# A two-layer trunk on one core: the order in which down blocks add to x, and four more seven-product pairs

## The chip, the cores and the metric

One core of a Trainium2 chip runs one program. The metric is the device time of one execution in microseconds (us); lower is better. The kernel works on 256 tokens, and nearly all of its time goes into multiplying these by large weight matrices that are read once from memory.

## What is computed

The reference is a decoder trunk of two layers in float32 for x of shape (1, 256, 2048):

```python
for layer in range(DEPTH):
    xn = rms_norm(x, norm_mix[layer])
    if layer % 2 == 0:
        x = x + mixer_mlstm_ssd(xn, *mixer_params[layer])
    else:
        x = x + mixer_moba(xn, *mixer_params[layer])
    x = x + swiglu(rms_norm(x, norm_ffn[layer]), *ffn_params[layer])
return rms_norm(x, final_norm)

def swiglu(x, w_gate, w_up, w_down):
    return (jax.nn.silu(x @ w_gate) * (x @ w_up)) @ w_down
```

The change concerns the two `swiglu` parts, with a hidden width of 5632. The mixers (an mLSTM and a Mamba-2 group in layer 0, block-sparse attention in layer 1) stay as they are.

## The kernel before, in words

**Products.** All float32 products are made from a high part (`wh`, rounded to the type fp32r by ScalarE, L269) and the rest (`wl`, made by VectorE, L274). So each product is three matmuls: high x high, high x low, low x high (L305 to L307 of `add`).

**Blocks.** A block multiplies the 256 tokens (two tiles of 128) by two strips of 512 weight columns, so it has four results, each in a PSUM bank: F[0] to F[3] (`acc_f`, banks 0 to 3), F[2 t + s] for token tile t and strip s. The inner dimension is taken in pairs of 128 rows; each letter of a block's plan in `PLAN` is one pair. "P" is a plain pair: four results x two halves of the pair x three matmuls, 24 in all, results in the order 0, 2, 1, 3. "S" is a pair with seven products in place of eight (Strassen's scheme), 21 matmuls. Three of its products go straight into F[0] to F[2], and four into E banks (`acc_e`, banks 4 to 7). It needs sums of the activations (`sk`, made by `activation_sums`) and of the weights (`sums`). In the FFN the weight sums are made by transfers that accumulate in memory order: SP loads one part (L259), POOL issues another that is added (L260); two more weight tiles are formed on VectorE (L287, L289).

**Behind the last S pair** of a block the E banks are combined into four SBUF tiles `pre` (one on ScalarE at L338, four instructions on VectorE at L339 to L342). `pre` and F together give the block's result: F[i] + pre[i], with a minus for i = 2. `pre` comes from the pool `tmp`, which has nine buffers.

**Hidden and down blocks.** `ffn` walks over eleven strips of 512 hidden columns in groups of 4, 4 and 3. For each strip `hidden` runs a block of eight pairs on gate and up (plan "x0" for the first strip of a layer, "x" for the others) and makes h from it; its results come out through `gathered`, which puts F[i] + pre[i] into `pre` (L388) at high priority. Then `down` multiplies the group's strips by the down matrix in two blocks, q = 0 and q = 1, one for each half of x's columns: plans "down4" (eight pairs) and "down3" (six). Their results are added to x (`xin`) by `add_all`, at L919: once for the four tiles of `pre`, once for the four banks F. There are twelve down blocks. The very last one (layer 1, group of three, q = 1) is the tail: it takes two pairs at a time at its end and adds its banks one by one in `finish_last`, together with the final norm.

**Order.** The program is written in one order; a scheduler then fixes the order of each engine's queue ahead of the run, by its own estimates. Each instruction's rank comes from its place in the program. `tc.high_priority(offset=n)` moves it forward by n places. Weights are prepared at offset 800, the combinations of E and the adds of F at 1600. Within a queue an engine runs strictly as written.

**Deferred work.** `later(n, ...)` puts off small work (above all `transpose_split`, which turns finished parts of x or h into the next blocks' operand) by n pairs. It runs in `tick()`, after each pair. Between the first and the last S of a block it is held back (`held`), because it uses the same banks 4 to 7.

Of the kernel before, what the change touches and what calls it, by code (L numbers as in the profile page):

```python
# [23 lines left out]
STRIP = 512  # L24
# [12 lines left out]
PLAN = {  # L37
    "bc": "PPPPPPPP", "xz": "PPPPPPPP", "qk0": "PPPPPPPP", "w1": ("PSPSPSPP", "PSPSPSPP"),
    "v0": "PPPSPSPP", "o": "PPPSPSPP", "qk1": "PPPSPSPP", "v1": "PPPSPSPP", "w2": ("PPPSPSPP", "PPPSPSPP"),
    "x": "PSPSPSSP", "x0": "PPPSPSPP", "down4": ("PSPSPSSP", "PSPSPSSP"), "down3": ("PSPSPP", "PPPSPP"),  # L40
    "av0": "PPPSPSPP", "aq": "PPPSPSPP", "av1": "PPPSPSPP", "wo": ("PPPPPPPP", "PPPSPSPP"),
}

# [18 lines left out]
def hybrid_trunk(ctx: ExitStack, tc: tile.TileContext, a: dict, out: bass.AP):  # L62
# [23 lines left out]
    def t2(shape, name, dt=F32):  # L86
        return tmp.tile(shape, dt, tag="tmp", name=name, bufs=9)
# [71 lines left out]
    last, cast, nth, fresh = [None], [None], [None], [None, None]  # L159
# [85 lines left out]
    def turn_strip(kt, s, src, gcol, wait, step=0):  # L245
        for i in range(2):
            later(wait + i * step, (kt.name, 2 * s + i), transpose_split, kt, 2 * s + i,
                  [x[:, i * T:(i + 1) * T] for x in src], gcol)
# [133 lines left out]
    def gathered(F, pre):  # L382
        for i in (0, 2, 1, 3):
            if pre is None:
                yield i // 2, i % 2, F[i]
            else:
                with tc.high_priority(offset=1600):
                    (nc.vector.tensor_sub if i == 2 else nc.vector.tensor_add)(pre[i], F[i], pre[i])  # L388
                yield i // 2, i % 2, pre[i]
# [34 lines left out]
    def first_pair(src, turns_after, warm):  # L424
        raw = []
        for w, col in src:
            raw.append(home("raw")([P, 2, STRIP], "raw"))
            nc.sync.dma_start(raw[-1], w[:2 * P, col:col + STRIP].rearrange("(a p) f -> p a f", p=P))
        b = xt0.pair(0)
        pt = aux_bank("p_tr")  # L430
        with tc.issue_after(turns_after):
            for i in range(2):
                for t in range(NT):
                    turned = nc.tensor.transpose(pt[:, i * T + t * P:i * T + (t + 1) * P],
                                                 xin[t][:, i * P:(i + 1) * P], ident).ins
        with tc.issue_after(turned):
            warm_up(warm)
        pair = pt.rearrange("p (a b) -> p a b", a=2)
        high = [home("wh")([P, 2, STRIP], "wh", F32R) for _ in raw]
        low = [home("wl")([P, 2, STRIP], "wl", F32R) for _ in raw]  # L440

        def staged(s, k):
            with tied(last[0], cast[0]):
                split(high[s][:, k, :], low[s][:, k, :], raw[s][:, k, :])
            cast[0], last[0] = fresh

        for k in range(2):
            g = pv[:, G_MIX0 + k:G_MIX0 + k + 1]
            with tied(last[0], cast[0]) if k else ExitStack():
                split(b[:, k, 0, :], b[:, k, 1, :], pair[:, k, :], g)  # L450
            cast[0], last[0] = fresh
            staged(0, k)
        for k in range(2):
            staged(1, k)
        return [[(h[:, k, :], l[:, k, :]) for k in range(2)] for h, l in zip(high, low)]
# [57 lines left out]
    with tc.high_priority(offset=2000):  # L513
        first = first_pair(((w_in, C_B), (w_in, C_C)), rows_turned, WARM[1])
# [383 lines left out]
    def ffn(xt, r, wg_, wu_, wd, name, finish, begin=None):  # L898

        def hidden(hT, i, s, plan):  # L900
            F, pre = block(((wg_, s * STRIP), (wu_, s * STRIP)), xt, 0, plan)
            got = {(t, i): src for t, i, src in gathered(F, pre)}
            hs = []
            for t in range(NT):
                g, u = got[t, 0], got[t, 1]
                h = t2([P, STRIP], "h")
                nc.scalar.activation(h, g, AF.Silu, scale=r[:, t:t + 1])
                nc.vector.scalar_tensor_tensor(h, u, r[:, t:t + 1], h, op0=OP.mult, op1=OP.mult)
                hs.append(h)
            turn_strip(hT, i, hs, None, 1)  # L910

        def down(hT, first, n, last):
            for q in range(2):
                c0 = 2 * q * STRIP
                dst = [xr_[t][:, c0 + n_ * STRIP:c0 + (n_ + 1) * STRIP] for t in range(NT) for n_ in range(2)]

                def add_all(what, minus=None):
                    for i, (d, x) in enumerate(zip(dst, what)):
                        (nc.vector.tensor_sub if i == minus else nc.vector.tensor_add)(d, d, x)  # L919

                if last and begin is not None:
                    begin(2 * q)
                    begin(2 * q + 1)
                tail = last and q and name == "b"
                F, _ = block(((wd, c0), (wd, c0 + STRIP)), hT, first * STRIP, PLAN[f"down{n}"][q], lambda pre: add_all(pre, 2),
                             lead=2 if tail else 1, order=(0, 1, 2, 3) if tail else (0, 2, 1, 3))
                if tail:
                    finish_last(F)
                    continue
                with tc.high_priority(offset=1600):  # L930
                    add_all(F)
                if last:
                    for s in (2 * q, 2 * q + 1):
                        finish(s)

        in_transfers[0] = True
        first = 0
        for n in (4, 4, 3):
            over = s_home if n == 3 else sk_home
            hT = KT(f"h{name}{first}", 4 * n, s_home, {1: s_home, 3: over, 5: over, 6: s_home})  # L940
            hT.sums = {j: None for j in range(2 * n) if "S" in [p[j] for p in PLAN[f"down{n}"]]}
            for i in range(n):
                hidden(hT, i, first + i, PLAN["x" if first + i else "x0"])
            down(hT, first, n, first + n == DFF // STRIP)
            first += n
        in_transfers[0] = False
# [207 lines left out]
```

## Time and profile before

| what | value |
|---|---|
| median of three runs | 2567.0 us (2564.78 to 2567.02) |
| the profiled execution's own time | 2565.22 us |
| its span, first to last instruction | 2563.4 us |
| TensorE busy | 2541.0 us (99%) |
| VectorE (DVE) busy | 2226.2 us (87%) |
| ScalarE (ACT) busy | 1562.7 us (61%) |
| POOL busy | 276.4 us (11%) |
| read from memory | 586.17 MB |

PE is TensorE, DVE VectorE, ACT ScalarE; SP and POOL issue transfers. A row of the timeline gives the start and the duration in us, the engine, the source line, the operation, `out<-in` by tile names, the shape and the count; in brackets stands idle time before it and what ended that. Matmuls are pipelined, so the row of one overlaps the next, and the distance between two starts is what a product takes. A row of the windows gives the stretch, its length, then for PE, PEld (weight loads), DVE, ACT and POOL the busy time and the number of instructions that touch the stretch, then the granted TensorE clock (1.00 is full), the busy share of the DMA engines, and GB/s.

### The profile page before, as it was taken

The numbers are of one execution on the slowest core, as the hardware profiler recorded it, in microseconds if no ns is written. First come the engines' busy times: TensorE is split into PE (matmuls) and PEld (weight loads), VectorE is DVE, ScalarE is ACT, GpSimd is POOL, SyncE is SP. The second block draws the span as 40 slices with busy tenths as digits, with TensorE's granted clock in tenths as the row PEclk, the third lists the DMA queues.
The fourth block names the chain that finished last, engine by engine and source line by source line (L and its number), as shares of the span: only waits on it lengthen the run. The fifth ranks groups of instructions, "written<-read, shape, count | busy, mean of one in ns | idle before, by whom it ended". The sixth has DMA issues, their size and how long they took to land.

```text
span 2563.4 us, 33984 instructions
## 1 busy us (share of the span) xinstructions
PE 2541.0 (99%) x11607; PEld 2092.0 (82%) x11607; DVE 2226.2 (87%) x2979; ACT 1562.7 (61%) x2100; POOL 276.4 (11%) x348
## 2 busy tenths in 40 slices
PE   9999999999999999999999999999999999999998
PEld 7888888888888888788878888888888878887887
DVE  6877789887788999999999988887889999999898
ACT  6566765565666665666556655646666656665664
POOL 2101200000001111111111000000011111111110
PEclk9999999999999999999999999999999999999999
DMA  8656656566477999999999756455679999999894
GB/s 281 182 167 186 205 166 218 172 195 203 164 230 217 280 265 283 264 282 261 288 264 281 224 179 205 157 165 181 205 234 268 275 276 268 274 273 298 253 262 162
DMA packets 310366, 590.58 MB, mean 230 GB/s; under 512 B 23928, under 2 KB 26496, under 8 KB 310192
## 3 DMA queue, kind: packets, MB, share of 16 engines
q1 hardware_dynamic: 270608, 514.07, 60.7%
q0 software_dynamic: 38400, 72.49, 15.9%
q8 instruction: 91, 1.49, 0.2%
q10 hardware_dynamic: 1184, 1.84, 0.2%
q14 instruction: 83, 0.68, 0.1%
HBM read 586.17 MB, written 2.14 MB: 229 GB/s over the span
## 4 chain that ended last, share of the span: by engine, by line
PE 95%; DVE 2%; DMA 1%; issue 1%; ACT 0%; POOL 0%; SPq 0%; POOLq 0%; DVEq 0%; ACTq 0%
PE acc_f L305 25%; PE acc_f L307 25%; PE acc_f L306 25%; PE acc_e L305 5%; PE acc_e L307 5%; PE acc_e L306 5%; PE p_tr L215 2%; PE p_y L727 1%; DVE wl L274 1%; DVE xin L919 1%; ACT wh L269 0%; PE p_qt L772 0%; DMA raw<-in_l_ffn_down 0%; DMA raw<-in_l_ffn_up 0%; PE p_num L815 0%
## 5 line engine op out<-in xcount | busy, mean ns | idle before, releaser
L269 ACT CAST wh<-raw 128x1024 fp32r<-128x1024 f32 (+1 forms) x1066 | 1037.8, 988 | 695.1 <-PE acc_f L307 314.9
L274 DVE TENSOR_TENSOR wl<-raw,wh 128x1024 fp32r<-128x1024 f32 (+1 forms) x1066 | 1203.7, 1143 | 233.2 <-ACT wh L269 222.2
L305 PE MATMUL acc_f<-wh,x 128*128 128x512 f32 x1216 | 477.8, 393 | 5.3 <-DVE xin L919 5.3
L306 PE MATMUL acc_f<-wl,x 128*128 128x512 f32 x1216 | 477.0, 392 | 0.8 <-DVE wl L274 0.8
L307 PE MATMUL acc_f<-wh,x 128*128 128x512 f32 x1216 | 475.6, 392 | 0.0
L305 PE MATMUL acc_f<-wh,xa 128*128 128x512 f32 x708 | 281.2, 397 | 1.3 <-ACT wh L145 1.3
L307 PE MATMUL acc_f<-wh,xa 128*128 128x512 f32 x708 | 276.5, 391 | 0.0
L306 PE MATMUL acc_f<-wl,xa 128*128 128x512 f32 x708 | 276.3, 390 | 0.0
L305 PEld LDWEIGHTS acc_f<-wh,x 128*128 128x128 f32 x1216 | 228.9, 188 | 53.6 <-DVE xin L919 7.0
L306 PEld LDWEIGHTS acc_f<-wl,x 128*128 128x128 f32 x1216 | 228.8, 188 | 49.0 <-DVE wl L274 2.5
L307 PEld LDWEIGHTS acc_f<-wh,x 128*128 128x128 f32 x1216 | 228.9, 188 | 46.8
L269 ACT CAST wh<-sums 128x1024 fp32r<-128x1024 f32 x156 | 164.1, 1052 | 135.8 <-PE acc_f L307 82.2
L274 DVE TENSOR_TENSOR wl<-sums,wh 128x1024 fp32r<-128x1024 f32 x156 | 190.2, 1219 | 21.0 <-ACT wh L269 21.0
L260 POOL DMA_DIRECT2D sums<-in_l_ffn_gate x84 | 72.8, 866 | 1162.3 <-DVE wl L274 525.6
L305 PE MATMUL acc_e<-wh,sk 128*128 128x512 f32 x468 | 185.1, 396 | 0.0
L306 PE MATMUL acc_e<-wl,sk 128*128 128x512 f32 x468 | 182.7, 390 | 0.0
L307 PE MATMUL acc_e<-wh,sk 128*128 128x512 f32 x468 | 181.7, 390 | 0.0
L307 PEld LDWEIGHTS acc_f<-wh,xa 128*128 128x128 f32 x708 | 132.9, 188 | 28.3
L305 PEld LDWEIGHTS acc_f<-wh,xa 128*128 128x128 f32 x708 | 133.0, 188 | 27.4 <-ACT wh L145 1.5
L306 PEld LDWEIGHTS acc_f<-wl,xa 128*128 128x128 f32 x708 | 133.2, 188 | 26.8 <-DVE wl L146 0.4
L305 PEld LDWEIGHTS acc_e<-wh,sk 128*128 128x128 f32 x468 | 87.8, 188 | 26.8 <-ACT xg L221 6.1
L289 DVE TENSOR_TENSOR raw<-raw 128x512 f32<-128x512 f32 x156 | 107.0, 686 | 1.9
(337 smaller groups left out, 3969.2 us busy)
## 6 DMA issues: line engine op xcount, KB each, us to landing
raw<-in_l_w_in SPq DMA_DIRECT2D x192, 512.0 KB, 4.3
raw<-in_l_ffn_gate SPq DMA_DIRECT2D x176, 512.0 KB, 6.2
raw<-in_l_ffn_down SPq DMA_DIRECT2D x138, 512.0 KB, 6.2
raw<-in_l_w_qkv SPq DMA_DIRECT2D x96, 512.0 KB, 4.6
raw<-in_l_ffn_up SPq DMA_DIRECT2D x92, 512.0 KB, 6.6
sums<-in_l_ffn_up SPq DMA_DIRECT2D x168, 256.0 KB, 4.3
raw<-in_l_w_out SPq DMA_DIRECT2D x64, 512.0 KB, 4.8
sums<-in_l_ffn_gate POOLq DMA_DIRECT2D x84, 256.0 KB, 6.8
```

The lines of the kernel that those rows point to most:

```text
L215: turned = nc.tensor.transpose(pt[:, i * T + t * P:i * T + (t + 1) * P], src[t][:, i * P:(i + 1) * P], ident)
L260: nc.gpsimd.dma_start(sums[:, i, :], other, accum_op=OP.add)
L269: cast[0] = nc.scalar.copy(h[:, :n, :], of[:, :n, :]).ins
L274: last[0] = nc.vector.tensor_sub(l[:, :n, :], of[:, :n, :], h[:, :n, :].bitcast(F32)).ins
L289: nc.vector.tensor_add(a[:, 0, :], a[:, 0, :], b[:, 1, :])
L305: nc.tensor.matmul(dst, ah, bh, start=start, stop=False, **kw)
L306: nc.tensor.matmul(dst, ah, bl, start=False, stop=False, **kw)
L307: nth[0] = nc.tensor.matmul(dst, al, bh, start=False, stop=stop, **kw).ins
L727: nc.tensor.matmul(py[:, o0:o0 + SHD], e[:, lo:lo + P], y[:, st, hs], start=st == 0, stop=st == t, skip_group_check=True)
L919: (nc.vector.tensor_sub if i == minus else nc.vector.tensor_add)(d, d, x)
```

## The change

It has two parts. In `down`, the block no longer gets a function that adds `pre` as soon as it is combined, except in the tail. Behind the block the banks F are added first (offset 1600, as before) and `pre` behind them: at offset 400, or 1600 in the last group of a layer. Before, the adds of `pre` stood ahead of those of F in the program, without an offset. And in `PLAN` one P becomes an S in two plans: pair 6 of "x0" and pair 1 of the second "down3"; each is used once per layer.

```diff
-    "x": "PSPSPSSP", "x0": "PPPSPSPP", "down4": ("PSPSPSSP", "PSPSPSSP"), "down3": ("PSPSPP", "PPPSPP"),
+    "x": "PSPSPSSP", "x0": "PPPSPSSP", "down4": ("PSPSPSSP", "PSPSPSSP"), "down3": ("PSPSPP", "PSPSPP"),
...
-                tail = last and q and name == "b"
-                F, _ = block(((wd, c0), (wd, c0 + STRIP)), hT, first * STRIP, PLAN[f"down{n}"][q], lambda pre: add_all(pre, 2),
+                tail = bool(last and q and name == "b")
+                plan = PLAN[f"down{n}"][q]
+                early = tail
+                F, pre = block(((wd, c0), (wd, c0 + STRIP)), hT, first * STRIP, plan,
+                               (lambda pre: add_all(pre, 2)) if early else None,
                              lead=2 if tail else 1, order=(0, 1, 2, 3) if tail else (0, 2, 1, 3))
                 if tail:
                     finish_last(F)
                     continue
                 with tc.high_priority(offset=1600):
                     add_all(F)
+                if not early:
+                    with tc.high_priority(offset=1600 if last else 400):
+                        add_all(pre, 2)
                 if last:
                     for s in (2 * q, 2 * q + 1):
                         finish(s)
```

## The prediction

> **What bounds the kernel now.** I read the page first, then TensorE's waits, then both sides of one block boundary in order of time.
>
> ```profile
> span 2563.4 us, 33984 instructions
> PE 2541.0 (99%) x11607; PEld 2092.0 (82%) x11607; DVE 2226.2 (87%) x2979; ACT 1562.7 (61%) x2100; POOL 276.4 (11%) x348
> ```
>
> TensorE is the bound: busy for 99% of the span. So there are only two ways to gain: fewer products, or fewer of TensorE's pauses. VectorE at 87% is the engine to watch. The waits of TensorE alone (total us, times, longest):
>
> ```profile
> PE acc_f L305 <- DVE xin L919: 8.9, 8, 2.5
> PE acc_f L306 <- DVE wl L274: 1.5, 8, 0.3
> PE acc_f L305 <- DVE pre L388: 0.3, 1, 0.3
> ```
>
> The largest is for L919, the line of `add_all`, which the change rewrites: eight times a product had no free bank, because a plain bank had not yet been added to x. Eight is also the number of down4 blocks (two strips of four, two halves, two layers); down3 blocks do not appear. One boundary, TensorE:
>
> ```profile
> 974.60 0.39 PE L305 MATMUL acc_e<-wh,sk 128*128 128x512 f32 x1
> 975.05 0.39 PE L307 MATMUL acc_e<-wh,sk 128*128 128x512 f32 x1
> 976.63 0.39 PE L305 MATMUL acc_f<-wh,ha 128*128 128x512 f32 x1
> ...
> 986.73 0.50 PE L306 MATMUL acc_f<-wl,ha 128*128 128x512 f32 x1 [0.18 <-DVE wl L274]
> 987.77 0.39 PE L307 MATMUL acc_f<-wh,ha 128*128 128x512 f32 x1
> 989.06 0.50 PE L305 MATMUL acc_f<-wh,ha 128*128 128x512 f32 x1 [0.91 <-DVE xin L919]
> ```
>
> From 974.60 to 976.63 are nine starts, 0.226 us each: that, not the 0.39 of one row, is the price of a product. The bracket therefore understates a pause: 987.77 to 989.06 is 1.29, so 1.06 is lost. VectorE at the same place:
>
> ```profile
> 974.12 0.68 DVE L919 TENSOR_TENSOR xin<-xin,pre 128x512 f32<-128x512 f32 x1
> 978.19 0.68 DVE L919 TENSOR_TENSOR xin<-xin,acc_f 128x512 f32<-128x512 f32 x1
> 986.59 0.68 DVE L919 TENSOR_TENSOR xin<-xin,pre 128x512 f32<-128x512 f32 x1
> 987.19 1.22 DVE L274 TENSOR_TENSOR wl<-raw,wh 128x1024 fp32r<-128x1024 f32 x1
> 988.33 0.68 DVE L919 TENSOR_TENSOR xin<-xin,acc_f 128x512 f32<-128x512 f32 x1
> 988.92 0.69 DVE L287 TENSOR_TENSOR raw<-raw,sums 128x512 f32<-128x512 f32 x1
> 989.53 1.28 DVE L919 TENSOR_TENSOR xin<-xin,pre 128x512 f32<-128x512 f32 x2
> 990.73 1.28 DVE L919 TENSOR_TENSOR xin<-xin,acc_f 128x512 f32<-128x512 f32 x2
> ```
>
> The last combined product of the block starts at 975.05; three products of its pair and the 24 of the plain pair follow, so the block ends at about 975.05 + 28 x 0.226 = 981.4, and its banks are full, in the order 0, 2, 1, 3, at 977.3, 978.7, 980.0 and 981.4. Bank 0 is added at once (978.19). Bank 1 is added only at 988.33, 8 us after it was full, since each `xin<-xin,acc_f` stands behind the `xin<-xin,pre` on the same part of x, and the pre adds have the lowest standing on VectorE: weight lows (L274) go before them. TensorE meanwhile does later work that needs no bank (so it needs later weights sooner: the 0.18 wait on `wl`), then stops.
>
> **The control.** Hidden blocks have the same plan, but `gathered` (L388) evacuates their plain banks at high priority and puts the lower-ranked work (L908) behind:
>
> ```profile
> 851.29 0.68 DVE L388 TENSOR_TENSOR pre<-acc_f,pre 128x512 f32<-128x512 f32 x1
> 854.22 1.88 DVE L388 TENSOR_TENSOR pre<-acc_f,pre 128x512 f32<-128x512 f32 x3
> 856.01 0.68 DVE L287 TENSOR_TENSOR raw<-raw,sums 128x512 f32<-128x512 f32 x1
> 864.52 0.75 DVE L908 SCALAR_TENSOR_TENSOR h<-pre,r,h 128x512 f32<-128x512 f32 x1
> ```
>
> This is what the changed down block should look like, and the L388 row of TensorE's waits shows what is left there: one wait of 0.3 us in the whole program.
>
> **Part 1, order of the adds.** No instruction is added; four L919 adds on plain banks move ahead of four on `pre`, in the eleven down blocks that are not the tail. I price it by counting products in 10 us windows: first a piece of a block without a pause, then seven boundaries, the stretch after a hidden boundary, and the eighth boundary.
>
> ```profile
> 970.00:980.00 10.00, 10.00 (x45) 8.29 (x45) 9.20 (x13) 7.21 (x8) 1.72 (x2) 1.00 1.00 282
> 985.00:995.00 10.00, 8.91 (x38) 6.70 (x37) 9.25 (x13) 3.92 (x5) 1.76 (x2) 1.00 1.01 279
> 1027.00:1037.00 10.00, 8.92 (x39) 6.69 (x38) 9.30 (x14) 4.09 (x4) 1.75 (x2) 1.00 0.97 276
> ...
> 2320.00:2330.00 10.00, 8.93 (x38) 6.72 (x37) 9.27 (x13) 3.95 (x5) 1.73 (x2) 1.00 1.02 306
> 855.00:865.00 10.00, 10.00 (x46) 8.29 (x45) 9.73 (x12) 6.45 (x7) 1.75 (x2) 1.00 0.76 230
> 2364.00:2374.00 10.00, 7.19 (x23) 5.30 (x23) 7.03 (x10) 1.44 (x2) 1.75 (x2) 0.83 0.91 292
> 2369.00:2373.00 4.00, 4.00 (x12) 3.17 (x11) 1.28 (x3) 1.04 (x1) 0.00 (x0) 0.57 0.95 221
> ```
>
> Where nothing waits, 45 or 46 products touch a window. Seven boundaries have 38 or 39 (three shown; all seven lose alike), so 7 products are missing: 7 x 0.226 = 1.6 us each, 11.1 for seven. It holds the main wait (1.06), the one on `wl` (0.35 with its hidden part) and slower starts behind both. The eighth has 23: 22.5 x 0.226 = 5.1 us. There the pause was 2.5 us by the waits, and the granted clock fell to 0.57 over the next 4 us, which is 4 x 0.43 = 1.7 of the 5.1. Sum: 16.2 us.
>
> The Trainium skill ("TensorE: Matmul & The Clock Gate", Part 1) says that the clock halves after an idle window of about 3.4 us, the window running free. Here 2.5 us sufficed, so the trace does not agree with the need for a wholly idle window. By that rule the 1.7 would have another origin and would stay; the gain would be 1.7 less.
>
> Can VectorE do it? A plain add now waits only for its bank's last product (L307). Queued behind it on VectorE stand the weight lows (L274), and TensorE waits for those. The next block needs the banks 4.1 us after they are full (18 products), against 0.68 for an add and 1.22 for a low ahead of it: about 2 us of room. The pre adds, 4 x 0.60 = 2.4 us a block by their spacing, are covered by VectorE's free time as now; without that cover they would cost up to 2.4 us x 11 = 26 as later lows. I take 0, the nearest row being L908 at 864.52, which does the same job beside 46 products without a pause. The four `pre` buffers are held a few us longer; the next block fills its own only behind its own last seven-product pair.
>
> At layer ends the pre adds get the high offset too: in the three down3 blocks concerned (q=0 twice, q=1 of layer 0) up to 2.4 us come ahead of lows. No pause stands there now, so nothing is to be won; a loss is between 0 and 2.4 each. I take 0, since two plain pairs (48 x 0.226 = 10.8 us) lie between the combinations and the block's end.
>
> **Part 2, four pairs.** A plain pair is 24 products, a seven-product pair 21. x0 (pair 6) and down3 q=1 (pair 1) run once per layer: 4 x 3 x 0.226 = 2.7 us off TensorE. What comes instead lies beside it. VectorE: two more sums (L287, L289, 0.69 each) and 3.5 instead of 2 lows of 1.22: 3.2 us a pair. ScalarE: 1.5 more casts of about 1.0. The activation sums exist already, since later blocks use them. Transfers, from
>
> ```profile
> raw<-in_l_ffn_gate SPq DMA_DIRECT2D x176, 512.0 KB, 6.2
> sums<-in_l_ffn_up SPq DMA_DIRECT2D x168, 256.0 KB, 4.3
> sums<-in_l_ffn_gate POOLq DMA_DIRECT2D x84, 256.0 KB, 6.8
> ...
> 800.00:840.00 40.00, 40.00 (x182) 33.13 (x181) 36.24 (x46) 24.20 (x28) 3.50 (x4) 1.00 0.84 243
> 920.00:960.00 40.00, 40.00 (x180) 32.51 (x179) 37.52 (x47) 24.30 (x29) 6.96 (x8) 1.00 0.96 276
> 2320.00:2360.00 40.00, 38.93 (x171) 31.56 (x170) 35.60 (x42) 21.48 (x24) 6.94 (x8) 1.00 0.97 280
> 2520.00:2563.00 43.00, 35.35 (x168) 29.58 (x166) 32.76 (x52) 17.92 (x31) 1.62 (x2) 0.97 0.29 107
> ```
>
> A plain pair loads 2 x 512 KB; a seven-product pair loads two sums on SP, two accumulating ones on POOL, and 512 + 256 KB raw: 1792 KB, so 768 KB (0.79 MB) more, about 2.9 us of transfers at 270 GB/s. Around x0 the transfers fill 0.84 and VectorE 36.2 of 40; the stretch with the full plan (920 to 960) stands 0.96 and 37.5 with no pause on TensorE, so x0 with three such pairs stays below what already runs. At the tail the share is 0.29. SP's and POOL's queues get two and two issues more, less one raw half; nothing is moved past them.
>
> One thing is displaced: in layer 0 the two transposed pairs of strip 1 were due after pair 1 of down3 q=1. Now pair 1 starts the held stretch, so they run after pair 4, near the end of the block. They are needed at pair 2 of the next block, one and two pairs later (3 x 24 x 0.226 = 16 us). Cost 0, upper end 2 us on a crowded VectorE. In the tail block the stretch after the last combined product is unchanged, so its 0.7 us passes straight to the end.
>
> **The sum.** 16.2 + 2.7 = 18.9 us, less about 1 for small new waits of the 0.3 kind: 18. The profiled execution took 2565.2 us (span 2563.4), 1.8 below the median 2567.0. 2565.2 - 18 = 2547; against the median 2549. I take 2548. The runs shown spread over 0.1%, so 0.2%, 5 us, is about what can be told from no change.
>
> **The rivals.**
> *The wait moves.* Banks come free in time, but four plain adds together hold up the lows, and TensorE waits on `wl` at each of the eight boundaries. Against it: the four L388 between 851.29 and 856.1 do that without a wait. For it: down blocks add x at fp32 twice, and 9.25 of 10 us of VectorE are taken at the boundary. If 1.1 us remains at each, 9 of the 16 are lost: 2557.
>
> *The order does not change.* The scheduler could place plain adds where they stand now, if it believes that VectorE has no room. Against it: nothing in their data holds them any more, and bank 0, whose pre add was early, went in at 978.19 at once. Then only the pairs count, less a little: 2564.
>
> *Slower: transfers become the bound.* The eight stretches already show shares of 0.91 to 1.02 in 10 us windows and 0.97 over 40. If the transfers cannot run faster, a block keeps its length whatever TensorE does, the 16 us do not appear, and each of the four pairs costs its 2.9 us of transfers: 2567 + 4 x 2.9 = 2578. It decides once the share is 1.0 over a whole block. Against it: hidden blocks move the same bytes per product at 0.96 and lose nothing.
>
> **How the numbers follow.** The forecast (2545 to 2551) has 0.66, the moved wait (2551 to 2560) 0.18, the unchanged order 0.10, the transfers 0.06. The range to 2560 leaves out the last two and a little above the first; its lower end is the lowest run shown, 2564.8, less 18.9, and 2 for fewer late weights in the last strips: 2544. Faster by over 0.2%: 0.84; within: 0.10; slower: 0.06.
>
> **What would show it.** Right: L919 gone from TensorE's waits, or under 1 us; windows at the ends of down4 blocks with 45 products; all `xin<-xin,acc_f` within 3 us of their bank's last product, ahead of three of the four `xin<-xin,pre`; granted clock 1.00 throughout the second half; 12 matmuls fewer in the page; 3.1 MB more transferred. Wrong: waits on `wl` above 5 us in total, waits on raw transfers at TensorE, or a pause near the end of layer 0.

## The result and the profile after

| | before | changed |
|---|---|---|
| median | 2565.89 us (2563.51 to 2567.02, four runs) | 2547.64 us (2547.07 to 2552.8, four runs) |
| profiled execution / span | 2565.22 / 2563.4 us | 2547.64 / 2545.9 us |

The ratio is 0.9935, with a 95% interval of 0.9917 to 0.9952: 17 us less, between 12 and 21. The forecast was 2548. The total came out right. Of its two terms the larger, the order of the adds, held; of the 2.7 us for the four pairs at most some 1.7 is seen, as the experiments show.

The page of the changed kernel, its first lines:

```profile
span 2545.9 us, 34058 instructions
PE 2534.9 (100%) x11595; PEld 2090.3 (82%) x11595; DVE 2236.4 (88%) x2995; ACT 1571.5 (62%) x2108; POOL 283.7 (11%) x356
```

There are 12 products fewer (11607 before), and VectorE has four more instructions per new pair (2995 against 2979, 10.2 us of work in all). The transfers moved 593.72 MB against 590.58, the 3.1 MB more that were forecast. All of TensorE's waits above the view's bound, in the changed kernel:

```profile
PE warm L122 <- POOL phase L105: 1.0, 1, 1.0
PE acc_f L305 <- ACT wh L269: 0.8, 1, 0.8
PE p_cols L645 <- ACT colsrc L635: 0.4, 1, 0.4
PE acc_e L305 <- DVE x L149: 0.3, 1, 0.3
```

L919 is gone, and so are the eight waits on `wl`. Two waits that were not there before stand in their place, 1.1 us together: a weight cast and a bank of the E group. Small waits of this kind differ from execution to execution of one kernel, as shown below. The first down4 boundary on VectorE, changed kernel:

```profile
977.04 0.68 DVE L919 TENSOR_TENSOR xin<-xin,acc_f 128x512 f32<-128x512 f32 x1
978.24 0.68 DVE L342 TENSOR_TENSOR pre<-pre,acc_e 128x512 f32<-128x512 f32 x1
978.84 1.31 DVE L919 TENSOR_TENSOR xin<-xin,acc_f 128x512 f32<-128x512 f32 x2
980.07 1.22 DVE L274 TENSOR_TENSOR wl<-raw,wh 128x1024 fp32r<-128x1024 f32 x1
981.20 0.68 DVE L919 TENSOR_TENSOR xin<-xin,acc_f 128x512 f32<-128x512 f32 x1
...
990.27 0.69 DVE L919 TENSOR_TENSOR xin<-xin,pre 128x512 f32<-128x512 f32 x1
994.35 0.69 DVE L919 TENSOR_TENSOR xin<-xin,pre 128x512 f32<-128x512 f32 x1
996.09 1.29 DVE L919 TENSOR_TENSOR xin<-xin,pre 128x512 f32<-128x512 f32 x2
```

All four banks are emptied within 5 us, and the adds of `pre` come 9 to 15 us after the last bank, between weight lows. The windows behind two boundaries, the last of the eight, and the place where the clock had fallen:

```profile
980.00:990.00 10.00, 10.00 (x46) 8.29 (x45) 9.77 (x12) 5.27 (x7) 1.76 (x2) 1.00 1.01 301
1021.00:1031.00 10.00, 10.00 (x46) 8.29 (x45) 9.77 (x11) 5.25 (x6) 1.76 (x2) 1.00 0.83 257
2347.00:2357.00 10.00, 10.00 (x46) 8.28 (x45) 10.00 (x13) 7.35 (x8) 0.83 (x2) 1.00 1.04 322
2369.00:2373.00 4.00, 4.00 (x20) 3.30 (x19) 3.13 (x5) 1.68 (x2) 0.00 (x0) 1.00 1.10 271
```

Each of the first three holds the 46 products that a hidden boundary holds; before there were 38, 39 and, at the eighth, 23. In the last stretch, of 4 us, 20 products stand where 12 stood. The Trainium skill ("Perfetto Trace Analysis", Optimizing Tensor Performance, Matmuls) says that independent groups of products should rotate through the banks, so that emptying one overlaps the next group's products. The traces agree: the 1.6 us at a boundary disappears when the bank is emptied by 981.9 and not by 989.0.

### The profile page after: what moved, and what is told of

The parts are those of the page before. It is cut to its first block, busy times and chain, and to the rows that moved or that the text cites. A ratio compares the mean times of both kernels' runs of the same rounds, so it can differ in the third digit from the quotient of the medians.

```text
span 2545.9 us, 34058 instructions
## 1 busy us (share of the span) xinstructions
PE 2534.9 (100%) x11595; PEld 2090.3 (82%) x11595; DVE 2236.4 (88%) x2995; ACT 1571.5 (62%) x2108; POOL 283.7 (11%) x356
## 2 busy tenths in 40 slices
DMA packets 312158, 593.72 MB, mean 233 GB/s; under 512 B 24184, under 2 KB 26752, under 8 KB 311984
## 4 chain that ended last, share of the span: by engine, by line
PE 94%; issue 3%; DVE 2%; DMA 1%; ACT 0%; POOL 0%; POOLq 0%; DVEq 0%; ACTq 0%
PE acc_f L305 24%; PE acc_f L307 24%; PE acc_f L306 24%; PE acc_e L305 6%; PE acc_e L307 5%; PE acc_e L306 5%; PE p_tr L215 1%; PE p_y L727 1%; DVE wl L274 1%; PE p_qt L772 0%; PE p_num L815 0%; DMA raw<-in_l_ffn_down 0%; PE p_cv L468 0%; PE p_o L1036 0%; PE p_qk L1008 0%
## 5 line engine op out<-in xcount | busy, mean ns | idle before, releaser
L274 DVE TENSOR_TENSOR wl<-raw,wh 128x1024 fp32r<-128x1024 f32 (+1 forms) x1070 | 1206.5, 1142 | 203.7 <-ACT wh L269 193.0
L305 PE MATMUL acc_f<-wh,x 128*128 128x512 f32 x1204 | 472.2, 392 | 0.0
L306 PE MATMUL acc_f<-wl,x 128*128 128x512 f32 x1204 | 471.2, 391 | 0.0
L307 PE MATMUL acc_f<-wh,x 128*128 128x512 f32 x1204 | 471.0, 391 | 0.0
L307 PEld LDWEIGHTS acc_f<-wh,x 128*128 128x128 f32 x1204 | 226.2, 188 | 46.4
L305 PEld LDWEIGHTS acc_f<-wh,x 128*128 128x128 f32 x1204 | 226.3, 188 | 45.8
L274 DVE TENSOR_TENSOR wl<-sums,wh 128x1024 fp32r<-128x1024 f32 x160 | 195.3, 1221 | 18.4 <-ACT wh L269 18.4
L305 PE MATMUL acc_e<-wh,sk 128*128 128x512 f32 x480 | 190.2, 396 | 0.0
L307 PE MATMUL acc_e<-wh,sk 128*128 128x512 f32 x480 | 186.5, 391 | 0.0
L287 DVE TENSOR_TENSOR raw<-raw,sums 128x512 f32<-128x512 f32 x160 | 109.6, 685 | 7.9 <-DMA sums<-in_l_ffn_down 4.9
```

The costliest lines, as they stand in the source:

```text
L274: last[0] = nc.vector.tensor_sub(l[:, :n, :], of[:, :n, :], h[:, :n, :].bitcast(F32)).ins
L287: nc.vector.tensor_add(b[:, 1, :], b[:, 0, :], sums[:, 0, :])
L305: nc.tensor.matmul(dst, ah, bh, start=start, stop=False, **kw)
L306: nc.tensor.matmul(dst, ah, bl, start=False, stop=False, **kw)
L307: nth[0] = nc.tensor.matmul(dst, al, bh, start=False, stop=stop, **kw).ins
```

## The experiments

Each was run beside the kernel before on the same chip; ratios are to it. Four chips were used, on which the kernel before had medians of 2564.3 to 2565.7 us, so medians of different rows can be told apart to about 1 us at best.

| run | median us | ratio (95%) |
|---|---|---|
| order only | 2548.64 | 0.9933 (0.9919 to 0.9946) |
| pairs only | 2565.06 | 0.9997 (0.9988 to 1.0006) |
| `pre` first, but high | 2554.47 | 0.9953 (0.9941 to 0.9965) |
| changed, `pre` high everywhere | 2552.45 | 0.9951 (0.9939 to 0.9963) |
| before, without the gain's loads | 2560.94 | 0.9984 (0.9976 to 0.9993) |
| order and x0's pair | 2546.2 | 0.9928 (0.9916 to 0.9941) |
| order and down3's pair | 2547.58 | 0.9933 (0.992 to 0.9947) |
| order only, through `gathered` | 2548.02 | 0.9936 (0.9923 to 0.9948) |
| changed, once more | 2546.99 | 0.9931 (0.9917 to 0.9945) |
| changed, last group's `pre` at 400 | 2546.99 | 0.993 (0.9917 to 0.9942) |
| changed, more transfers (misplaced) | 2547.25 | 0.9931 (0.9919 to 0.9943) |
| changed, more transfers in down4 | 2553.24 | 0.9955 (0.9942 to 0.9969) |

**Order only, and pairs only.** The two parts apart: the changed `down` with the old `PLAN`, and the old `down` with the new one.

> The changed order of the adds with the old plans (no new seven-product pair). Theory A, that the plain banks stood behind the adds of pre and nothing else cost the time at the eight down4 boundaries: 14 to 17 us less than before (about 2550), TensorE's waits for L919 gone, 11607 products. Rival B, that part of the gain of the whole change comes from the pairs by more than their 12 products: less than 12 us gained here.

> The four seven-product pairs with the old order of the adds. Theory A: 12 products of 0.226 us, so 2.7 us less than before (about 2563), and the eight waits for L919 stay at about 9 us in the table of TensorE's waits. Rival B: more than 5 us gained. Rival C, that transfers or VectorE pay for the pairs: no gain, or up to 8 us slower, with new waits on wl or raw in the first block of an FFN or in the last down block.

The order alone gives 16.7 us by the medians; the forecast's term was 16.2. TensorE's waits in the run with the order alone, all that are listed:

```profile
PE warm L122 <- POOL phase L105: 1.0, 1, 1.0
PE p_cols L645 <- ACT colsrc L635: 0.4, 1, 0.4
PE p_tr L215 <- DVE h L908: 0.2, 1, 0.2
```

L919 is gone without any new pair. Where the time went can be read place by place: both kernels run the same 11607 products in nearly the same order, so the start of the n-th product in one trace can be set beside that of the n-th in the other. From one side of a boundary to the other the run with the order alone gains 1.7 us at each of seven boundaries and 5.0 at the eighth, 16.9 in all. The two executions differ by 18.2; the other 1.3 us lie elsewhere, 0.7 of them ahead of the first FFN, where the change does nothing.

The pairs alone give 0.3 by the medians (0.8 by the ratio; the interval reaches from 3.1 less to 1.5 more). Waits of the run with pairs only:

```profile
PE acc_f L305 <- DVE xin L919: 8.6, 8, 2.3
PE acc_f L306 <- DVE wl L274: 1.6, 8, 0.3
```

As expected, the boundaries are untouched. So part 1 is nearly all of the gain. That the pairs bring 2.7 us is not shown; the interval of this run alone does not rule it out either.

**Standing or place?** The adds of `pre` stay ahead, as before, with a high offset:

```diff
+                def add_pre(pre):
+                    with tc.high_priority(offset=0 if tail else 1600):
+                        add_all(pre, 2)
...
-                F, _ = block(..., PLAN[f"down{n}"][q], lambda pre: add_all(pre, 2),
+                F, _ = block(..., PLAN[f"down{n}"][q], add_pre,
```

> The kernel before with one edit: the adds of pre stay ahead of those of F but get offset 1600 (but for the tail). Theory A in the form that the low standing of the pre adds was the cause, not their place ahead: the waits for L919 go and 12 to 16 us are gained, nearly as with the changed order. Rival D, that it is the place: each plain bank still waits for a pre add, and these for the combinations, so at least 0.5 us stays at each of eight boundaries and the gain is under 12 us.

10.9 us were gained, under the 12 of theory A: rival D is right in part. TensorE's waits in this run, and VectorE at the first boundary that has one:

```profile
PE acc_f L305 <- DVE xin L919: 3.0, 4, 1.0
```

```profile
1021.22 0.68 DVE L341 TENSOR_TENSOR pre<-pre,acc_e 128x512 f32<-128x512 f32 x1
1021.81 0.68 DVE L342 TENSOR_TENSOR pre<-pre,acc_e 128x512 f32<-128x512 f32 x1
1022.41 1.29 DVE L919 TENSOR_TENSOR xin<-xin,pre 128x512 f32<-128x512 f32 x2
1023.62 1.88 DVE L919 TENSOR_TENSOR xin<-xin,acc_f 128x512 f32<-128x512 f32 x3
```

Three banks wait until the combinations and two more adds of `pre` are through. At four of the eight boundaries, those ahead of a hidden block, TensorE still waits, up to 1.0 us. Set beside the run with the order alone, product by product, this run loses 0.7 to 1.3 us at each of these four, 4.1 in all: that is the place ahead. Another 1.1 us go at 2343, where TensorE waits for a weight low and VectorE had waited 3.4 us for late weight sums. So the low standing was most of the cause (10.9 of 16.7 us), the place ahead is worth about 4, and the rest, under 2, is lost at no bank; the next run, which has the same high offset and nothing ahead of the banks, loses time of this kind too.

**What the adds behind cost.** In the changed kernel, `pre` gets the high offset in every block:

```diff
-                    with tc.high_priority(offset=1600 if last else 400):
+                    with tc.high_priority(offset=1600):
```

> The changed kernel with offset 1600 for the pre adds in every down block, so that 4 x 0.60 us more of VectorE's work come ahead of weight lows at the eight down4 boundaries. Theory A with its price of 0 (two pairs of lows lie ready): within 1 us of the changed kernel, about 2548, no wait on wl above 0.5 us. Rival E, the wait moves: TensorE waits for wl 0.5 to 2.4 us at each boundary, 4 to 19 us slower than the changed kernel.

It took 5 us longer than the changed kernel (2547.64 and 2546.99), the lower end of rival E in time. TensorE's waits:

```profile
PE acc_f L306 <- DVE wl L274: 1.8, 5, 0.9
PE p_tr L215 <- DVE h L908: 1.7, 3, 0.6
```

But the waits do not stand where rival E put them, at each boundary. Set beside the changed kernel, product by product, only 1.5 of the 5.0 us go within some 15 us behind a boundary (0.6 each at the second and the fourth). The others go at some ten places further on, most of them 30 to 50 us behind one. VectorE waits more for late weights; its largest row of this kind, first in the changed kernel and then here:

```profile
DVE raw L287 <- DMA sums<-in_l_ffn_down: 4.9, 3, 2.5
DVE raw L287 <- DMA sums<-in_l_ffn_down: 8.7, 4, 3.2
```

All rows of this kind for the FFN weights (L287 and L274) add up to 7.7 us there, 23.3 here and 20.2 in the run before, which has the high offset too; in the other runs with the changed order they are 4.8 to 8.5, but for the one with more transfers in place below. One such sum is issued by POOL at 1002.00 and not at 999.20, when VectorE is through with earlier weights, and lands at 1007.81 and not at 1005.36. This suggests that the four adds of 0.60 us hold up the weight lows, and with them the next loads, which come late some 25 us further on. That this makes up the whole of the 5 us is not shown. The 0 in the forecast holds only because the adds are put behind the lows.

**Only the bank.** The old plans, and down blocks emptied as hidden blocks are:

```diff
-                with tc.high_priority(offset=1600):
-                    add_all(F)
-                if not early:
-                    with tc.high_priority(offset=1600 if last else 400):
-                        add_all(pre, 2)
+                for t, i, src in gathered(F, pre):
+                    with tc.high_priority(offset=1600 if last else 400):
+                        nc.vector.tensor_add(dst[2 * t + i], dst[2 * t + i], src)
```

> The old plans, and down blocks evacuated as hidden blocks are: F and pre are added into pre at offset 1600, and x gets that sum later at 400 (1600 in the last group). Same number of VectorE instructions, but x is not touched to free a bank. Theory A, that only the time at which a bank comes free counts: the waits for the banks go, 14 to 17 us less than before, as with the changed order (2548.6 for order alone). Rival: x or the place of its adds matters in itself, and the time differs from the order-only run by more than 4 us.

2548.02, the order-only time within 0.6 us, no wait for a bank, and the same 16.9 us gained at the eight boundaries, product by product. VectorE, first boundary:

```profile
978.19 0.69 DVE L388 TENSOR_TENSOR pre<-acc_f,pre 128x512 f32<-128x512 f32 x1
981.12 1.88 DVE L388 TENSOR_TENSOR pre<-acc_f,pre 128x512 f32<-128x512 f32 x3
991.42 0.68 DVE L935 TENSOR_TENSOR xin<-xin,pre 128x512 f32<-128x512 f32 x1
```

Here x gets nothing before 991, and the gain is the same. So x and the order of the sums do not matter; when the bank comes free does.

**The eighth pause.** Before, the last boundary lost 5.1 us where the others lost 1.6. The kernel before, with one edit, which leaves out the final norm's gain:

```diff
-        nc.scalar.dma_start(gain[s], bass.AP(tensor=fsrc.tensor, offset=fsrc.offset + s * STRIP, ap=[[0, P], [1, STRIP]]))
+        nc.gpsimd.memset(gain[s], 1.0)
```

> The kernel before with the four loads of the final norm's gain left out (the gain is set to 1, so the final multiplication by it is left out). It asks why the eighth pause was 2.5 us and not 0.9. Theory F, late transfers: these loads share the transfers with the weights just ahead of that pause, VectorE's low or sum waits for a late weight, and the plain add behind it is late too: the eighth pause falls to about 0.9 us by the waits, the clock stays at 1.00 there, 3 us gained (about 2562). Rival G, the place in the queue: VectorE's order there has two pre adds ahead of the plain add, and the pause stays above 2 us; no gain.

The time fell by 4.7 us by the medians (4.1 by the ratio, 1.8 to 6.2), and the pause became like the others (TensorE, this run):

```profile
2365.39 0.40 PE L307 MATMUL acc_f<-wh,x 128*128 128x512 f32 x1
2366.69 0.50 PE L305 MATMUL acc_f<-wh,x 128*128 128x512 f32 x1 [0.90 <-DVE xin L919]
```

So with the gain's loads in the program the eighth pause is long. VectorE's rows say why, first before, then without the loads:

```profile
2361.36 4.29 DVE L274 TENSOR_TENSOR wl<-raw,wh 128x1024 fp32r<-128x1024 f32 x4
2365.86 0.69 DVE L287 TENSOR_TENSOR raw<-raw,sums 128x512 f32<-128x512 f32 x1 [0.21 <-DMA raw<-in_l_ffn_up]
2366.47 1.28 DVE L919 TENSOR_TENSOR xin<-xin,pre 128x512 f32<-128x512 f32 x2
2367.67 1.27 DVE L919 TENSOR_TENSOR xin<-xin,acc_f 128x512 f32<-128x512 f32 x2
```

```profile
2363.07 1.23 DVE L274 TENSOR_TENSOR wl<-raw,wh 128x1024 fp32r<-128x1024 f32 x1 [0.17 <-ACT wh L269]
2364.22 0.68 DVE L919 TENSOR_TENSOR xin<-xin,pre 128x512 f32<-128x512 f32 x1
2364.82 1.22 DVE L274 TENSOR_TENSOR wl<-raw,wh 128x1024 fp32r<-128x1024 f32 x1
2365.95 0.68 DVE L919 TENSOR_TENSOR xin<-xin,acc_f 128x512 f32<-128x512 f32 x1
```

VectorE waited only 0.21 us for a transfer. What made the bank late is the order of its queue: before, a weight sum and a second add of `pre` stood ahead of the bank's add as well. The run with pairs only has this same order there, no wait for a transfer, and a pause of 2.31 us. So theory F forecast the shorter pause, but not for the right cause: the place in the queue (rival G) makes the pause, and the edit shortened it because the scheduler, without the loads, put VectorE's queue in another order.

**Which pairs?** The changed order with one of the two new letters each:

> The changed order with the new pair in x0 alone. By the order-only run (2548.6) a pair should save 0.68 us and gives back 0.33 at the next block's start in the trace of the changed kernel: 0.7 us less, 2548; 6 products fewer; no new wait above 0.1 us. Rival: a new wait of 0.5 us or more appears and x0 costs time.

> The changed order with the new pair in the second down3 block alone. Theory H, that the pairs' gain is given back here: waits near the end of layer 0 (0.3 us on L149) and for a late cast in the last down blocks (0.8 us) come back as in the changed kernel, against 1.4 us for 6 products: within 1 us of the order-only run (2548.6). Rival: these waits were chance, and 1.4 us are gained (2547.3).

> The changed kernel once more beside the others: 2547 to 2549. With the order-only run (2548.6) and the run with x0's pair (2546.2) it tells what all four pairs bring on top of the order: theory H says within 1 us of the order-only run and above the run with x0's pair alone; the prediction's step said 2.7 us below the order-only run (2546).

With x0's pair alone 2546.2, the lowest median of all; with down3's alone 2547.58; with both 2547.64 and 2546.99; with none 2548.64. Against the kernel before on the same chip that is 19.5, 18.1, 18.2 and 17.3 us gained, and 16.7 with none. The intervals all overlap, so no order among these is shown by the times.

The traces tell more. Set beside the run with the order alone, each x0 pair saves 0.34 to 0.45 us of its 0.68 in all five traces that have both new letters or x0's alone: in layer 0, for one, three starts in the next block come 0.30 to 0.34 us behind the one before them, not 0.23. So the two x0 pairs save 0.7 to 0.8 us, and most of the 2.4 by the medians is not theirs. The down3 pair of layer 0 saves nothing: the five traces that have it lose 0.1 to 1.3 us there. The one in the tail brings 0.0 to 1.1, of which 0.3 shows with x0's letter alone too. All four together save 0.5 and 1.7 us in the two traces of the changed kernel. TensorE's waits with down3's pair alone:

```profile
PE acc_e L305 <- DVE x L149: 1.3, 2, 1.0
```

In layer 0 the S at pair 1 wants a bank of the E group just behind the transposes that used it, and TensorE waits until VectorE has split what they left there (L149): 1.0 us, at 1442.68. The other 0.3 stands at the first S of the block that follows, at 1484.59. Both are absent from the order-only profile; the second is present in the changed one, at 1482.86. Half of theory H holds (the end of layer 0). The late cast of 0.8 us is absent here and in the changed kernel's second profile; it comes and goes.

**The late cast.** The changed kernel with one edit:

```diff
-                    with tc.high_priority(offset=1600 if last else 400):
+                    with tc.high_priority(offset=1600 if last and name == "a" else 400):
```

> The changed kernel with offset 400 in place of 1600 for the pre adds of layer 1's last group (its first block; the tail is as it was). Theory I, that the 0.8 us wait for a cast in the last down blocks of the changed kernel comes from late transfers: it stays between 0.5 and 1.2 us in the profile, time as the changed kernel within 1 us. Rival, that the pre adds ahead of VectorE's lows cause it: the wait goes and about 1 us is gained.

2546.99, as the changed kernel, and no late cast in its profile. Since the changed kernel run again had none either, this run tells nothing on the cause. For transfers speaks the place of the first profile where the weights of the last blocks came in:

```profile
2482.00:2500.00 18.00, 18.00 (x84) 14.56 (x83) 15.75 (x19) 9.71 (x12) 1.76 (x2) 1.00 0.99 274
```

and that ScalarE's casts waited for the down weights, the longest time (5.3 us, until 2501.16) just ahead of the late cast:

```profile
ACT wh L269 <- DMA raw<-in_l_ffn_down: 31.1, 10, 5.3
```

In the second profile of the same kernel the cast at this place was released by a product, not by a load, at 2500.38.

**How near are the transfers?** Copies of weights to a scratch place in memory, unused, two a down4 block; then four, each tied behind the first raw load of a plain pair:

```diff
+        if extra[0] and not summed:
+            extra[0] -= 1
+            with tc.issue_after(loaded):
+                nc.sync.dma_start(drp.tile([P, 2, STRIP], F32, ...), pair(wa, ca))
```

> The changed kernel with two more transfers of 512 KB in each of the eight down4 blocks (weights copied to a scratch place in memory, not used): 1.05 MB on some 11.3 MB a block, 9% more. Theory J, that the shares of 0.94 to 0.98 leave at most 6%: transfers become the bound in these blocks, TensorE waits for casts or lows there, and the time rises by about 3% of 8 x 41 us, 5 to 15 us. Rival K, that the share overstates the load: no wait above 0.5 us and no change within 2 us, so transfers were never near to bounding the change.

> The run with more transfers put its copies 40 to 92 us after the start, far from the down4 blocks, and told nothing on them. Here each copy stands in SP's queue right behind the first raw load of a plain pair, in the eight down4 blocks alone, and there are four of 512 KB a block (2.1 MB on 11.3, 19%). Theory J, that the share of 0.96 to 0.99 is the load: 15 to 60 us slower, with TensorE waiting for wl or casts in these blocks. Rival K, that the share overstates the load and there is room for a fifth more: within 3 us of the changed kernel (2547).

The first is a miss: nothing held the copies back, and they ran long before the FFN:

```profile
L265 SPq DMA_DIRECT2D spill<-in_l_ffn_down x16: 553/561/1199, 39.9 to 91.5; - x16
```

The second costs 6 us, between both theories. Its profile is of the slowest of its five executions (2558.03 us). Two down4 blocks of the changed kernel, and then the same stretch with the copies:

```profile
940.00:1020.00 80.00, 80.00 (x356) 65.63 (x355) 75.05 (x90) 48.90 (x54) 13.95 (x16) 1.00 0.99 281
```

```profile
940.00:1020.00 80.00, 78.62 (x347) 63.83 (x346) 71.17 (x86) 45.81 (x52) 12.25 (x14) 1.00 1.02 307
PE acc_f L311 <- DVE wl L279: 5.0, 7, 0.9
```

With 19% more bytes asked for, the rate rose by 9%, from 281 to 307 GB/s, while the share went only from 0.99 to 1.02. In the other three such stretches (from 1190, 2015 and 2265) it rose from 287, 283 and 280 to 310, 314 and 320. So a share of 0.99 was not the end; about a tenth was left. Beyond it TensorE waits for lows at seven places, 5.0 us in all, and VectorE waits 21.5 us for late FFN weights, against 7.7. Whether the copies cost by their bytes or by their place in SP's queue, ahead of other loads, was not separated.

## Why the prediction was right, and where it was not

- **The bound and the place of the loss** held: eight boundaries, named by the line of `add_all`, and no others. Order only and `gathered` show it from two sides.
- **Part 1, 16.2 us**: 16.7 by the medians, 16.9 at the eight boundaries by the traces (1.7 each and 5.0, forecast 1.6 and 5.1). The count of products in 10 us windows was a better measure than the 8.9 us of the table of waits, which misses the part of a pause that a row's 0.39 us covers, the waits on `wl` and the slow starts. That it fits to half a microsecond is partly luck, since 1.7 of it is the clock, below.
- **"The pre adds have the lowest standing"** as the whole cause was too narrow: raising it gives 10.9 of 16.7; about 4 more need the banks ahead.
- **Price 0 for the adds behind**: right at offset 400. At 1600 they cost 5 us, so the rival of the moved wait was near in size, though most of it appeared as late loads and not at the boundaries; it was decided by where `pre` is ranked.
- **The weak step is the 2.7 us of part 2.** The products went (12 fewer), the time only in part: 0.5 to 1.7 us by the traces, 0.3 for the pairs alone by the medians. Of the 0.68 us of a pair, x0's keep about half, behind which the next block starts more slowly; the step took 0 for that. "Cost 0, upper end 2 us" for what layer 0's end displaces was wrong in its middle value: that pair loses 0.1 to 1.3 us net, with waits of 0.3 to 1.0 us for a bank of the E group, which is wanted at once behind the transposes. And "at the tail the share is 0.29" reads the wrong stretch: that row shows when the last products run, while most of their weights are asked for by 2500, in a stretch with a share of 0.99; in one of the two traces of the changed kernel the late cast there took the whole gain of the tail's pair. The sum's "about 1 for small new waits" covered half of this shortfall or more.
- **Slower by transfers** did not come; the run in place shows about a tenth of room. The 2.9 us of transfers that each pair was given in that rival fit into it.
- **The clock's 1.7 us.** It is gone from the changed profile (1.00 at 2369 to 2373). That it is lost at each such pause is not so: with pairs only, 2.3 us at the same place left the clock at 1.00, in the fastest of that run's eleven executions. The rows, before and with pairs only:

```profile
2368.40 0.50 PE L305 MATMUL acc_f<-wh,x 128*128 128x512 f32 x1 [2.55 <-DVE xin L919]
...
2367.89 0.50 PE L305 MATMUL acc_f<-wh,x 128*128 128x512 f32 x1 [2.31 <-DVE xin L919]
...
2368.00:2373.00 5.00, 5.00 (x22) 4.13 (x23) 3.33 (x5) 1.74 (x2) 0.86 (x1) 1.00 0.98 254
```

The mean granted clock on record of each execution hints at how often: it is below 0.999 in 37 of the 48 executions of the kernel before that ran beside the experiments, in 4 of 11 with pairs only, and in 1 of 49 of the kernels that empty the banks first. Half the clock for 3.4 us takes 0.0007 off that mean. So most executions before seem to have lost some clock, and the agreement of 16.2 with 16.7 rests on that; at which pause is not known for them.

## What to carry to other kernels

Where an accumulating bank feeds the next block, let no low-ranked work stand ahead of the instruction that empties it, neither in the queue nor in its data; put sums that need no bank behind the work that feeds TensorE. To price such a pause, count the products in equal windows against a neighbouring place of the same plan that does not wait. To see afterwards where a gain came from, set the n-th product of one trace beside the n-th of the other: that shows 0.3 us at a place where the times of whole executions spread over several. A saving of products is worth its time only where the weights, banks and casts of that very stretch have room, and the loads of a stretch run ahead of its products: look there for the share.

## What the runs showed of the hardware that I had not expected

A busy share of the transfer engines near 1.0 was no ceiling: 281 GB/s at 0.99 became 307 at 1.02 over the same 80 us. And a single pause did not always cost clock: after 2.55 us without products it was granted at half for 3.4 us (mean 0.57 over 4 us), after 2.31 us in another execution it stayed at full. Whether the length of the pause or its moment decides, two pauses cannot tell.
